# Key products of the next chunk pair traced between the two chunks of the current pair's scan

## The chip, the cores and the metric

One core of a Trainium2 chip runs the whole kernel; nothing is exchanged with other cores. The metric is the device time of one launch in microseconds (us), as the median of several runs.

## What is computed

Two layers of a backbone for a diffusion model, on 512 latent tokens and 256 context tokens of 1024 channels. Each layer has a mixer (an RWKV-7 recurrence in both directions, windowed attention, a Fourier mixer, merged by gates) and a gated ConvFFN. What this case touches is the recurrence, four heads of 64 channels, run forward and backward, over the context first and then over the latents:

```python
def wkv_scan(state0, feat, d, reverse):
    r, v, kk, decays, keys, removals, _ = feat

    def step(S, inp):
        r_t, w_t, k_t, v_t, kk_t, b_t = inp
        sa = jnp.einsum("bhvk,bhk->bhv", S, -kk_t)
        S = S * w_t[:, :, None, :] + sa[..., :, None] * b_t[..., None, :] + v_t[..., :, None] * k_t[..., None, :]
        return S, jnp.einsum("bhvk,bhk->bhv", S, r_t)

    xs = tuple(jnp.swapaxes(t, 0, 1) for t in (r, decays[d], keys[d], v, kk, removals[d]))
    S_last, y = lax.scan(step, state0, xs, reverse=reverse)
    return jnp.swapaxes(y, 0, 1), S_last
```

## The kernel before, in words

All activations stand with channels on the 128 partitions and tokens along the free dimension. The recurrence is done in chunks of 64 tokens, and two chunks of either direction make a *pair* (128 tokens). A layer has six pairs: w = 0 and 1 are the context, w = 2 to 5 the latents. Both directions and all heads of a pair go together. A pair has three parts.

- `wkv_features` (L779) computes the pair's operands for both directions d. Four small products a direction on TensorE (L814) give decay and gate; ScalarE takes tanh and exp; VectorE sums the decay along the chunk (L825) and multiplies the operands into the tiles W1 (L851 on VectorE, L853 on POOL) and BK (L854, L855). Then come the **key products**: for each direction and half of the partitions four products BK x W1 (L864) into one PSUM tile, whose masked copies go to MR (L869) and back into W1 (L870). POOL scales BK by the decay (L872).
- `wkv_inverse` inverts eight 64x64 unit triangular blocks that stand in MR. Its first half is VectorE's alone: a transpose of MR (L909), 30 small dependent steps that invert 16x16 blocks (L917 and L919, fifteen each), scaled copies (L924, L926) and two transposes (L929, L930). Its second half joins the blocks to 32 and to 64, by small products on TensorE (L938, L944, L948, L967, L974) and copies on VectorE and ScalarE between them (L940, L952, L957, L970, L977).
- `wkv_step`, once for each chunk j = 0, 1, carries the state: products L1021, copy L1024, products with the inverse L1028, copy L1031, products L1039, sum L1042 into the next chunk's state, and the outputs (L1047, L1052, L1063). `wkv_prep` (L987, L997) transposes a chunk's operands for it.

`wkv_scan` (L878) traces inverse, preparations and steps of pair w; before it the features of pair w + 1 are traced. All this is at high priority. At normal priority stands the *filler*: projections of the attention, Fourier and gate inputs, each of three products per weight tile (L177, L178, L179; 128x512, and in layer 0 128x256 too for the context), with weight splits on ScalarE (L106) and on POOL or VectorE (L118). The tile scheduler orders each engine's instructions by data, buffers and priority, and priority is the order of tracing; at run time each engine then works through its list in order. PSUM has two slots "x" for products, inverse and preparations and one slot "y" for the steps; MR has two buffers.

The run method's caller `mix` traces pair 0's scan before the projections and the others after them. What follows is built from the code:

Of the kernel before, what the change touches and what calls it, by code (L numbers as in the profile page):

```python
# [63 lines left out]
class Kern:  # L64
# [713 lines left out]

    def wkv_features(self, l, w, F, P, wp, wt):  # L779

        nc = self.nc
        x = P["x"]
        NC = 2
        WT = NC * CH
        W = {}
        MR = self.t(wp, [128, 4 * NC, 128], "MR", bufs=2)
        need_y = l == 0 or w > 1
        m = 128 if need_y else 64
        first = w in (0, 2, 3)
        part = "c" if w < 2 else "l"  # L790
        los = (w * WT, TC - (w + 1) * WT) if w < 2 else ((w - 2) * WT, TL - (w - 1) * WT)
        base = TL if w < 2 else 0

        def rows(t, h):
            return t[64 * h:64 * h + 64]

        for d in range(2):
            lo = base + los[d]

            def flip(s):  # L800
                return s[:, :, ::-1] if d else s

            def tok(t):
                return flip(t[:, :, lo:lo + WT])

            W1 = [self.t(wp, [128, NC, 2, 128], f"W1{h}", bufs=4) for h in range(2)]
            for h in range(2):

                nc.gpsimd.memset(rows(W1[h], 1 - h)[:, :, :, 0:m], 0.0)
            pp = self.ps()  # L810
            for z, (lw, xx) in enumerate(((P["w2"], F["xw"]), (P["a2"], F["xa"]))):
                for k in range(2):
                    c = (2 * z + k) * WT
                    nc.tensor.matmul(pp[:, c:c + WT], lhsT=lw[:, d, k * 128:(k + 1) * 128], rhs=xx[:, lo:lo + WT],  # L814
                                     start=True, stop=True)
            sw = self.t(wt, [128, 2, WT], "wt")
            ta = self.t(wt, [128, 2, WT], "wt")
            for z, (o, b, sc) in enumerate(((sw, 2 * d, 0.5), (ta, 4 + 2 * d, -0.5))):
                for k in range(2):
                    c = (2 * z + k) * WT  # L820
                    src = pp[:, c:c + WT]
                    self.act(o[:, k], src[:, ::-1] if d else src, AF.Tanh, scale=sc, bias=x[:, b + k:b + k + 1])
            self.sig(sw)
            L = self.t(wt, [128, 2, WT], "wt")
            nc.vector.tensor_tensor_scan(L.rearrange("p k t -> p (k t)"), self.smask, sw.rearrange("p k t -> p (k t)"),  # L825
                                         0.0, ALU.mult, ALU.add)

            kf = self.t(wt, [128, 2, WT], "wt")
            for k in range(2):
                self.act(kf[:, k], ta[:, k], AF.Identity, scale=x[:, 8 + k:9 + k], bias=x[:, 10 + k:11 + k])  # L830
            e1 = self.t(wp, [128, 2, NC, CH + 1], "e1", bufs=4)
            nc.gpsimd.memset(e1[:, :, :, 0:1], 1.0)
            self.act(e1[:, :, :, 1:], L.rearrange("p k (c t) -> p k c t", t=CH), AF.Exp, scale=-DECAY)
            e2 = self.t(wt, [128, 2, WT], "wt")
            self.act(e2, L, AF.Exp, scale=DECAY, bias=x[:, 25:26])
            nc.vector.tensor_tensor(kf, kf, tok(F["k"]), ALU.mult)
            na = ta
            nc.vector.scalar_tensor_tensor(na, ta, -1.0, tok(F["kk"]), ALU.add, ALU.mult)
            if need_y:
                kb = flip(F["kb" + part][:, :, los[d]:los[d] + WT])  # L840
                if first:
                    nc.gpsimd.tensor_copy(kb, kf)
                else:
                    nc.gpsimd.tensor_tensor(kb, kb, kf, ALU.add)
            BK = self.t(wp, [128, NC, 2, 128], "BK", bufs=4)
            split = lambda a: a.rearrange("p k (c t) -> p k c t", t=CH)
            for h in range(2):
                ww = rows(W1[h], h).rearrange("p c k t -> p k c t")
                bk = rows(BK, h).rearrange("p c k t -> p k c t")
                o = 64 * h  # L850
                nc.vector.tensor_tensor(ww[:, :, :, 0:64], split(rows(tok(F["kk"]), h)), rows(e1, h)[:, :, :, 0:64], ALU.mult)  # L851
                if need_y:
                    nc.gpsimd.tensor_tensor(ww[:, :, :, 64:128], split(rows(tok(F["r"]), h)), rows(e1, h)[:, :, :, 1:65], ALU.mult)  # L853
                nc.vector.tensor_tensor(bk[:, :, :, o:o + 64], split(rows(na, h)), split(rows(e2, h)), ALU.mult)  # L854
                nc.vector.tensor_tensor(bk[:, :, :, 64 - o:128 - o], split(rows(kf, h)), split(rows(e2, h)), ALU.mult)  # L855
            vs = self.t(wp, [128, 2, WT + CH], "vs_", bufs=4)
            nc.gpsimd.memset(vs[0:64, :, 0:64], 0.0)
            nc.gpsimd.memset(vs[64:128, :, WT:WT + 64], 0.0)
            self.act(vs[0:64, :, 64:64 + WT], tok(F["v"])[0:64])
            self.act(vs[64:128, :, 0:WT], tok(F["v"])[64:128])  # L860
            for h in range(2):
                ps = self.ps()
                for q in range(4):
                    nc.tensor.matmul(ps[:, q * 128:q * 128 + m], lhsT=BK[:, q // 2, q % 2, :],  # L864
                                     rhs=W1[h][:, q // 2, q % 2, 0:m], start=True, stop=True)
                pv = ps.rearrange("p (q t) -> p q t", q=4)[:, :, 0:m]
                oth = 1 - h
                mask = lambda z: rows(self.gmask, z)[:, 0:m].unsqueeze(1).broadcast_to((64, 4, m))
                nc.vector.tensor_tensor(rows(MR, h)[:, 4 * d:4 * d + 4, 0:m], rows(pv, h), mask(h), ALU.mult)  # L869
                nc.vector.tensor_tensor(rows(W1[h], oth).rearrange("p c k t -> p (c k) t")[:, :, 0:m], rows(pv, oth),  # L870
                                        mask(oth), ALU.mult)
            nc.gpsimd.tensor_tensor(  # L872
                BK, BK, e1[:, :, :, 64].rearrange("p k c -> p c k").unsqueeze(3).broadcast_to((128, NC, 2, 128)), ALU.mult)
            W[d] = (W1, BK, vs, e1)
        return w, W, MR, los

    def wkv_scan(self, l, win, then, F, S, wb):
        nc = self.nc  # L878
        w, W, MR, los = win
        NC = 2  # L880
        TTt = self.wkv_inverse(MR, wb)
        cur = S["cur"]
        if cur is None:
            cur = self.wkv_prep(0, W, wb)
            for h in range(2):
                nc.gpsimd.memset(cur[0][h][64 * h:64 * h + 64], 0.0)
        for j in range(NC):
            nxt = None
            if j + 1 < NC:
                nxt = self.wkv_prep(j + 1, W, wb)  # L890
            elif then is not None:
                nxt = self.wkv_prep(0, then[1], wb)
            self.wkv_step(l, w, j, F, W, MR, TTt, cur, nxt, wb, los)
            cur = nxt
        S["cur"] = cur

    def wkv_inverse(self, MR, wp):
# [431 lines left out]
    def mix(self, l, at, atp, W, pls, ring, A, B):  # L1329
# [7 lines left out]
        P = self.rwkv_params(l, rp)  # L1337
        F = {m: self.t(rp, [128, 2, TT], m) for m in ("r", "k", "v")}
# [26 lines left out]
        wa = self.pool("wa", side=B)  # L1365
        wt = self.pool("wt", bufs=6, side=B)
        wb = self.pool("wb", side=B)
        S = {"cur": None}
        with tc.high_priority():
            w0 = self.wkv_features(l, 0, F, P, wa, wt)  # L1370
            w1 = self.wkv_features(l, 1, F, P, wa, wt)
            self.wkv_scan(l, w0, w1, F, S, wb)

        stg = self.pool("stg", bufs=2 + l, side=B)
        cos = self.t(stg, [128, TL], "cos", bufs=1)
# [75 lines left out]
        work = fill()  # L1451
        with tc.high_priority():
            for w in range(2, 7):
                w0, w1 = w1, self.wkv_features(l, w, F, P, wa, wt) if w < 6 else None
                self.wkv_scan(l, w0, w1, F, S, wb)
            wb.release()
            wt.release()
            wa.release()
            tmp = self.pool("rtmp", side=B)
            self.rwkv_readout(l, F, P, y, tmp)  # L1460
            tmp.release()
# [346 lines left out]
```

## Time and profile before

| what | value |
|---|---|
| runs before | 2510.15 us median of 3 (2508.0 to 2512.45) |
| the profiled execution's own time | 2513.85 us |
| its span | 2511.9 us |
| TensorE busy (PE) | 2293.3 us, 91% |
| VectorE busy (DVE) | 1889.0 us, 75% |
| ScalarE (ACT), GpSimd (POOL) busy | 1052.8 and 965.1 us |
| mean granted TensorE clock | 0.965 |

PE is TensorE's matmuls and PEld its weight loads, DVE is VectorE, ACT ScalarE, POOL GpSimd. All times within the profile are counted from the start of its span. The scan of layer 0 lies at about 150 to 443 us and that of layer 1 at about 1541 to 1817 us. A granted clock of 1.00 is 2.4 GHz and one of 0.50 is 1.2 GHz; a mean over a stretch lies between them. In the rows, idle time before an instruction is followed by what ended it (the releaser). A row of the table of stretches gives its begin and end, its length, the busy time (and count of instructions) of PE, PEld, DVE, ACT and POOL, the mean granted clock, the DMA engines' busy share and GB/s. A row of a timeline gives start, duration, engine, line, operation, tiles and, in brackets, the idle time before it. A row of groups gives the count, then busy us and mean ns of one, then the idle us before them with its releasers. A row of waits gives who waited for whom, the sum of us, how often, and the longest.

### The profile page before, as it was taken

To read this page: it belongs to the slowest core of one execution; us is meant where nothing else is said; L and a number is where in the kernel's file an instruction comes from. 1 tells how busy PE (TensorE), PEld (TensorE's weight loads), DVE (VectorE), ACT (ScalarE), POOL (GpSimd) and SP (SyncE) were. 2 spreads that over 40 slices of the span, in tenths; PEclk is the share of its full clock that TensorE was granted. 3 is DMA by queue.
4 is the path that set the end of the run, shared out by engine and by line. 5 is a ranking of instruction groups with operands and counts; after the bars stand their busy time and mean duration, and the time that the engine had idled before them with its cause. 6 is when DMAs were issued, how large, how long until landed. Compare 5 with 4: busy or idle time off the path is not lost. (4 is left out here: it accounts for less than half of the span.)

```text
span 2511.9 us, 43604 instructions
## 1 busy us (share of the span) xinstructions
PE 2293.3 (91%) x16612; PEld 1923.1 (77%) x16612; DVE 1889.0 (75%) x3458; ACT 1052.8 (42%) x2153; POOL 965.1 (38%) x965
## 2 busy tenths in 40 slices
PE   7878999999999979999999989889889997899997
PEld 4757777887777768898898777667667776888886
DVE  4967777838866587778778854888667857989988
ACT  3234343335434444343333544435345434544443
POOL 4443322023332363333333544343224424644453
PEclk9989989999999989999999999899999998999999
DMA  7611111644334322222222322112275643322321
GB/s 241 190 51 47 57 37 46 204 146 122 118 122 125 104 67 65 63 72 68 64 69 66 122 93 63 54 59 61 76 211 149 195 128 113 117 88 85 98 89 59
DMA packets 284529, 251.36 MB, mean 100 GB/s; under 512 B 14524, under 2 KB 241300, under 8 KB 284320
## 3 DMA queue, kind: packets, MB, share of 16 engines
q1 hardware_dynamic: 284320, 248.58, 32.0%
q8 instruction: 131, 2.15, 0.4%
q14 instruction: 78, 0.64, 0.1%
HBM read 221.23 MB, written 27.29 MB: 99 GB/s over the span
## 5 line engine op out<-in xcount | busy, mean ns | idle before, releaser
L177 PE MATMUL mm<-at,wh 128*128 128x256 f32 (+2 forms) x1968 | 661.8, 337 | 14.4 <-DVE v L614 7.0
L178 PE MATMUL mm<-at,wh 128*128 128x256 f32 (+2 forms) x1968 | 660.5, 336 | 12.8 <-POOL at L118 7.3
L179 PE MATMUL mm<-at,wl 128*128 128x256 f32 (+2 forms) x1968 | 659.7, 336 | 8.2 <-DVE wl L118 5.9
L118 POOL TENSOR_TENSOR wl<-wr,wh 128x512 fp32r<-128x512 f32 (+1 forms) x248 | 341.8, 1385 | 466.2 <-ACT wh L106 444.0
L177 PEld LDWEIGHTS mm<-at,wh 128*128 128x128 f32 x1968 | 380.8, 194 | 46.9 <-issue 5.6
L178 PEld LDWEIGHTS mm<-at,wh 128*128 128x128 f32 x1968 | 381.1, 194 | 43.4 <-POOL at L118 10.0
L179 PEld LDWEIGHTS mm<-at,wl 128*128 128x128 f32 x1968 | 380.9, 194 | 34.4 <-DVE wl L118 8.9
L106 ACT ACTIVATE wh<-wr 128x512 fp32r<-128x512 f32 (+1 forms) x342 | 204.9, 605 | 235.2 <-PE mm L178 141.3
L118 DVE TENSOR_TENSOR wl<-ws,wh 128x512 fp32r<-128x512 f32 x176 | 166.8, 949 | 65.6 <-ACT wh L106 65.6
L177 PE MATMUL x<-dh,hid 128*128 128x512 f32 x440 | 178.0, 405 | 29.8 <-DVE acc L604 27.7
L295 DVE SCALAR_TENSOR_TENSOR ma<-mw,s,ma 128x256 f32<-128x256 f32 x336 | 187.3, 597 | 11.0 <-DMA mw<-in_mod_w 8.2
L179 PE MATMUL x<-dh,hid 128*128 128x512 f32 x440 | 173.3, 395 | 1.0 <-DVE hid L118 1.0
L178 PE MATMUL x<-dl,hid 128*128 128x512 f32 x440 | 173.2, 394 | 0.0
L604 DVE TENSOR_TENSOR acc<-x,acc 128x512 f32<-128x512 f32 x200 | 134.4, 682 | 24.2 <-PE x L179 23.7
L118 POOL TENSOR_TENSOR dl<-dr,dh 128x1024 fp32r<-128x1024 f32 x44 | 112.2, 2549 | 83.9 <-ACT dh L106 83.9
L106 ACT ACTIVATE wh<-ws 128x512 fp32r<-128x512 f32 x170 | 103.7, 623 | 84.9 <-PE mm L178 70.5
L177 PEld LDWEIGHTS x<-dh,hid 128*128 128x128 f32 x440 | 83.3, 189 | 56.4 <-DVE acc L604 38.6
L154 POOL TENSOR_TENSOR ws<-wr,wr 128x512 f32<-128x512 f32 x42 | 66.4, 1580 | 139.5 <-DVE wl L118 136.9
L178 PE MATMUL x<-at,wh 128*128 128x512 f32 (+2 forms) x312 | 114.4, 367 | 5.0 <-POOL at L118 3.1
L177 PE MATMUL x<-at,wh 128*128 128x512 f32 (+2 forms) x312 | 114.7, 368 | 0.9 <-DVE wh L114 0.7
L106 ACT ACTIVATE P<-P,st 128x513 f32<-128x513 f32 (+5 forms) x120 | 86.0, 722 | 69.8 <-DVE P L1234 58.6
L154 POOL TENSOR_TENSOR ws<-ws,wr 128x512 f32<-128x512 f32 x42 | 62.8, 1495 | 132.5 <-DVE wl L118 75.0
(490 smaller groups left out, 4859.0 us busy)
## 6 DMA issues: line engine op xcount, KB each, us to landing
mw<-in_mod_w SPq DMA_DIRECT2D x96, 512.0 KB, 4.1
wr<-in_ffn_up SPq DMA_DIRECT2D x176, 256.0 KB, 3.1
wr<-in_w_in SPq DMA_DIRECT2D x164, 256.0 KB, 3.0
dr<-in_ffn_down SPq DMA_DIRECT2D x44, 512.0 KB, 3.3
gd<-sg SPq DMA_DIRECT2D x32, 256.0 KB, 2.0
wraw<-in_w_out SPq DMA_DIRECT2D x32, 256.0 KB, 3.7
hd<-h SPq DMA_DIRECT2D x32, 256.0 KB, 2.4
h<-hd SPq DMA_DIRECT2D x28, 256.0 KB, 6.7
```

The costliest lines, as they stand in the source:

```text
L106: return self.nc.scalar.activation(out, in_, func, **kw)
L118: e.tensor_tensor(lo, full, hi.bitcast(F32), ALU.subtract)
L154: e.tensor_tensor(raw[m], raw[x], raw[y], op)
L177: mm(ps, lhsT=lh, rhs=rh, start=first and k == 0, stop=False)
L178: mm(ps, lhsT=lh, rhs=rl, start=False, stop=False)
L179: mm(ps, lhsT=ll, rhs=rh, start=False, stop=last and k == nk - 1)
L295: nc.vector.scalar_tensor_tensor(acc[s], mw[:, k % 4], v, acc[s], ALU.mult, ALU.add)
L604: nc.vector.tensor_tensor(acc[i][:, cs], ps, acc[i][:, cs], ALU.add)
```

## The change

`wkv_features` becomes a generator with two parts. It stops once the operand tiles W1, BK, vs and e1 of both directions are made, and the caller goes on with that. The key products, their evacuations into MR and W1 and the scaling of BK are its second part. For pair 0 the second part is traced at once. For every other pair `wkv_scan` traces it after the first of the two steps of the pair before. No operation is added or left out.

```diff
--- before.py
+++ after.py
@@ -778,6 +778,7 @@
 
     def wkv_features(self, l, w, F, P, wp, wt):
 
+
         nc = self.nc
         x = P["x"]
         NC = 2
@@ -858,6 +859,10 @@
             nc.gpsimd.memset(vs[64:128, :, WT:WT + 64], 0.0)
             self.act(vs[0:64, :, 64:64 + WT], tok(F["v"])[0:64])
             self.act(vs[64:128, :, 0:WT], tok(F["v"])[64:128])
+            W[d] = (W1, BK, vs, e1)
+        yield w, W, MR, los
+        for d in range(2):
+            W1, BK, _, e1 = W[d]
             for h in range(2):
                 ps = self.ps()
                 for q in range(4):
@@ -871,10 +876,9 @@
                                         mask(oth), ALU.mult)
             nc.gpsimd.tensor_tensor(
                 BK, BK, e1[:, :, :, 64].rearrange("p k c -> p c k").unsqueeze(3).broadcast_to((128, NC, 2, 128)), ALU.mult)
-            W[d] = (W1, BK, vs, e1)
-        return w, W, MR, los
-
-    def wkv_scan(self, l, win, then, F, S, wb):
+
+    def wkv_scan(self, l, win, then, rest, F, S, wb):
+
         nc = self.nc
         w, W, MR, los = win
         NC = 2
@@ -892,6 +896,8 @@
                 nxt = self.wkv_prep(0, then[1], wb)
             self.wkv_step(l, w, j, F, W, MR, TTt, cur, nxt, wb, los)
             cur = nxt
+            if j == 0:
+                self.advance(rest, 1)
         S["cur"] = cur
 
     def wkv_inverse(self, MR, wp):
@@ -1367,9 +1373,12 @@
         wb = self.pool("wb", side=B)
         S = {"cur": None}
         with tc.high_priority():
-            w0 = self.wkv_features(l, 0, F, P, wa, wt)
-            w1 = self.wkv_features(l, 1, F, P, wa, wt)
-            self.wkv_scan(l, w0, w1, F, S, wb)
+            f0 = self.wkv_features(l, 0, F, P, wa, wt)
+            w0 = next(f0)
+            self.advance(f0, 1)
+            f1 = self.wkv_features(l, 1, F, P, wa, wt)
+            w1 = next(f1)
+            self.wkv_scan(l, w0, w1, f1, F, S, wb)
 
         stg = self.pool("stg", bufs=2 + l, side=B)
         cos = self.t(stg, [128, TL], "cos", bufs=1)
@@ -1451,8 +1460,9 @@
         work = fill()
         with tc.high_priority():
             for w in range(2, 7):
-                w0, w1 = w1, self.wkv_features(l, w, F, P, wa, wt) if w < 6 else None
-                self.wkv_scan(l, w0, w1, F, S, wb)
+                f1 = self.wkv_features(l, w, F, P, wa, wt) if w < 6 else None
+                w0, w1 = w1, next(f1) if w < 6 else None
+                self.wkv_scan(l, w0, w1, f1, F, S, wb)
             wb.release()
             wt.release()
             wa.release()
```

The built programs show where the instructions go. The lists below are each engine's own, in its order; the change shifts line numbers after L779 by up to ten, so L915 is the former L909, L946 the former L940, L983 the former L977, L1037 the former L1031, L874 and L875 the former L869 and L870.

VectorE, layer 1, the start of the scan, before: the evacuations of pair 0's first direction (`MR`, `W`), the features of its second one (`wt`, `kk`, `BK`). L1148 and L1150 are filler.

```order
L869 TENSOR_TENSOR MR_15447<-x_15488,table_539 64x4x64
L870 TENSOR_TENSOR W_2990_15448<-x_15488,table_539 64x4x64
L869 TENSOR_TENSOR MR_15447<-x_15495,table_539 64x4x64
L870 TENSOR_TENSOR W_2991_15449<-x_15495,table_539 64x4x64
L1148 TENSOR_TENSOR mm_16118<-mm_16118,sin_15986 128x512
L1150 TENSOR_TENSOR stg_15988<-stg_15988,mm_16118 128x512
L726 TENSOR_SCALAR wt_15512<-wt_15512 128x256
L825 SCALAR_TENSOR_TENSOR wt_15519<-smask_543,wt_15512 128x256
L836 TENSOR_TENSOR wt_15521<-wt_15521,k_14903 128x256
L838 SCALAR_TENSOR_TENSOR wt_15513<-wt_15513,kk_15416 128x256
L851 TENSOR_TENSOR W_3003_15503<-kk_15416,e_3010_15524 64x2x2x64
L854 TENSOR_TENSOR BK_15531<-wt_15513,wt_15527 64x2x2x64
```

After, the same place:

```order
L855 TENSOR_TENSOR BK_15516<-wt_15498,wt_15512 64x2x2x64
L856 TENSOR_TENSOR BK_15516<-wt_15506,wt_15512 64x2x2x64
L874 TENSOR_TENSOR MR_15447<-x_15528,table_539 64x4x64
L875 TENSOR_TENSOR W_2990_15448<-x_15528,table_539 64x4x64
L874 TENSOR_TENSOR MR_15447<-x_15535,table_539 64x4x64
L875 TENSOR_TENSOR W_2991_15449<-x_15535,table_539 64x4x64
L1154 TENSOR_TENSOR mm_16118<-mm_16118,sin_15986 128x512
L874 TENSOR_TENSOR MR_15447<-x_15543,table_539 64x4x64
L875 TENSOR_TENSOR W_3001_15488<-x_15543,table_539 64x4x64
L874 TENSOR_TENSOR MR_15447<-x_15550,table_539 64x4x64
L875 TENSOR_TENSOR W_3002_15489<-x_15550,table_539 64x4x64
L915 STREAM_TRANSPOSE iv_15639<-MR_15447 128x512
```

The second direction's features are done before the first evacuation, all of pair 0's evacuations follow each other, and the transpose L915 that starts its inverse comes right behind them. Before, that transpose stood behind the second direction's features and its own evacuations.

VectorE, layer 1, the end of the inverse of pair 4 and the step it feeds, before: `TTt_17852` is that inverse, `itmp` and `T_3405` belong to the small steps of pair 5's inverse, and `XV` is written by the first step.

```order
L977 COPY TTt_17852<-x_17946 32x8x32
L917 TENSOR_TENSOR itmp_18136<-F_3404_18134,T_3405_18135 128x63
L919 TENSOR_TENSOR T_3405_18135<-T_3405_18135,itmp_18136 128x9x7
L917 TENSOR_TENSOR itmp_18136<-F_3404_18134,T_3405_18135 128x64
L919 TENSOR_TENSOR T_3405_18135<-T_3405_18135,itmp_18136 128x8x8
L917 TENSOR_TENSOR itmp_18136<-F_3404_18134,T_3405_18135 128x63
L1031 COPY XV_3334_17622<-y_18008 64x256
L919 TENSOR_TENSOR T_3405_18135<-T_3405_18135,itmp_18136 128x7x9
L917 TENSOR_TENSOR itmp_18136<-F_3404_18134,T_3405_18135 128x60
L919 TENSOR_TENSOR T_3405_18135<-T_3405_18135,itmp_18136 128x6x10
```

After, the same place (`TTt_17822` is pair 4's inverse, `MR_17690` belongs to pair 5):

```order
L946 COPY Ps_17826<-x_17827 128x128
L958 SCALAR_TENSOR_TENSOR iv_17823<-x_17827,table_539,iv_17823 32x8x16 x2
L963 COPY TTt_17822<-x_17827 16x8x16
L976 COPY Pb_17915<-x_17916 32x256
L963 COPY TTt_17822<-x_17827 16x8x16
L983 COPY TTt_17822<-x_17916 32x8x32
L1037 COPY XV_3334_17622<-y_17978 64x256
L874 TENSOR_TENSOR MR_17690<-x_18028,table_539 64x512
L875 TENSOR_TENSOR W_3343_17691<-x_18028,table_539 64x512
L1048 TENSOR_TENSOR ZV_3378_17958<-y_17999,Zp_17973 64x256
L1048 TENSOR_TENSOR ZV_3379_17959<-y_17999,Zp_17973 64x256
```

No small step of the next inverse stands among the copies of this one any more. The evacuations of pair 5's key products, which its inverse reads, now stand behind the first step's copy into `XV`.

TensorE, layer 1, the second half of pair 4's inverse, before (`mm` is filler, `x_17857` and `x_17946` are the inverse's PSUM tiles):

```order
L938 MATMUL x_17857<-iv_17853,MR_17247 32x16 x32
L178 MATMUL mm_18878<-at_14639,wh_18874 128x512
L179 MATMUL mm_18878<-at_14638,wl_18875 128x512
L177 MATMUL mm_18878<-at_14640,wh_18874 128x512
L178 MATMUL mm_18878<-at_14641,wh_18874 128x512
L944 MATMUL x_17857<-Ps_17856,TTt_17852 32x16 x16
L948 MATMUL x_17857<-TTt_17852,Ps_17856 16x16 x32
L179 MATMUL mm_18878<-at_14640,wl_18875 128x512
L177 MATMUL mm_18878<-at_14642,wh_18874 128x512
L178 MATMUL mm_18878<-at_14643,wh_18874 128x512
L179 MATMUL mm_18878<-at_14642,wl_18875 128x512
L967 MATMUL x_17946<-iv_17853,MR_17247 32x32
```

After, the same place:

```order
L177 MATMUL mm_18958<-at_14644,wh_18954 128x512
L178 MATMUL mm_18958<-at_14645,wh_18954 128x512
L179 MATMUL mm_18958<-at_14644,wl_18955 128x512
L944 MATMUL x_17827<-iv_17823,MR_17247 32x16 x32
L950 MATMUL x_17827<-Ps_17826,TTt_17822 32x16 x16
L954 MATMUL x_17827<-TTt_17822,Ps_17826 16x16 x32
L973 MATMUL x_17916<-iv_17823,MR_17247 32x32 x16
L980 MATMUL x_17916<-TTt_17822,Pb_17915 32x32 x16
L993 MATMUL x_17953<-ident_61,vs__3292_17286 128x128 x2
L993 MATMUL x_17953<-ident_61,vs__3303_17329 128x128 x2
L1034 MATMUL y_17978<-q_3386_17987,TTt_17822 64x64
```

Before, filler stands between the inverse's products to the end of the scan: 20 such matmuls from the first L938 to the last L1028 of pair 4. After, there are 15 in pairs 1 to 3 and none in pairs 4 and 5: the matmul ahead of pair 4's inverse is the last of the 516 of layer 1's scan, of which 165 stand ahead of the first inverse. In layer 0 the order has 673 filler matmuls up to the end of the scan before, 721 after, and 89 of them now stand between the products of pair 0 and its inverse.

## Rows read from the trace of the kernel before

**Rows 1.** The page's first part: busy us, share of the span, instructions

```profile
PE 2293.3 (91%) x16612; PEld 1923.1 (77%) x16612; DVE 1889.0 (75%) x3458; ACT 1052.8 (42%) x2153; POOL 965.1 (38%) x965
```

**Rows 2.** Table of stretches, both scans

```profile
150.20:227.00 76.80, 57.21 (x538) 48.11 (x538) 63.53 (x141) 30.12 (x75) 30.05 (x41) 0.87 0.15 49
...
227.00:411.70 184.70, 170.35 (x2222) 138.58 (x2223) 137.14 (x328) 75.03 (x196) 63.73 (x116) 0.93 0.14 44
...
1541.00:1623.00 82.00, 69.35 (x552) 56.22 (x550) 58.33 (x138) 35.56 (x78) 26.85 (x29) 0.83 0.19 59
...
1746.20:1786.30 40.10, 37.63 (x522) 28.90 (x522) 35.38 (x87) 19.76 (x51) 13.92 (x24) 1.00 0.19 61
```

**Rows 3.** VectorE's groups, 1746.2 to 1786.2

```profile
L118 DVE TENSOR_TENSOR wl<-wr,wh 128x512 fp32r<-128x512 f32 x6 | 4.4, 730 | 0.3 <-issue 0.2
L917 DVE TENSOR_TENSOR itmp<-F,T 128x60 f32<-128x60 f32 (+7 forms) x15 | 3.4, 225 | 0.5
L919 DVE TENSOR_TENSOR T<-T,itmp 128x63 f32<-128x63 f32 (+7 forms) x15 | 3.2, 216 | 0.5
...
L869 DVE TENSOR_TENSOR MR<-x,table 64x512 f32<-64x512 f32 x4 | 2.7, 686 | 1.3 <-PE x L864 1.3
...
L825 DVE TENSOR_TENSOR_SCAN wt<-smask,wt 128x256 f32<-128x256 bf16 x2 | 1.4, 688 | 0.0
...
L1024 DVE COPY q<-y 128x256 f32<-128x256 f32 x2 | 0.8, 415 | 0.8 <-PE y L1021 0.8
```

**Rows 4.** VectorE's timeline, layer 1, inverse of pair 4 and its step

```profile
1755.56 1.09 DVE L929 STREAM_TRANSPOSE iv<-iv 128x512 f32<-128x512 f32 x1
...
1776.18 0.27 DVE L940 COPY Ps<-x 128x128 f32<-128x128 f32 x1
...
1786.26 0.42 DVE L1031 COPY XV<-y 64x256 f32<-64x256 f32 x1 [0.23 <-PE y L1028]
```

**Rows 5.** Table of stretches, L940 to L1031, covered by the next inverse

```profile
355.68:370.08 14.40, 13.15 (x206) 9.81 (x205) 7.87 (x26) 5.55 (x14) 0.80 (x4) 0.65 0.17 48
402.93:411.65 8.72, 8.72 (x210) 7.23 (x209) 7.52 (x26) 4.40 (x11) 0.00 (x0) 1.00 0.21 64
...
1776.18:1786.26 10.08, 10.08 (x205) 7.22 (x204) 8.86 (x31) 4.41 (x11) 0.00 (x0) 1.00 0.26 81
```

**Rows 6.** The same stretch in the last pair of layer 1 and of layer 0

```profile
1795.86:1807.19 11.33, 11.23 (x262) 8.50 (x262) 3.99 (x12) 4.62 (x12) 2.79 (x5) 1.00 0.16 49
422.73:432.86 10.13, 10.13 (x249) 8.06 (x248) 3.24 (x11) 3.75 (x10) 1.52 (x4) 1.00 0.09 29
```

**Rows 7.** Who VectorE waited for, 1541 to 1623: us in total, times, longest

```profile
DVE kk L775 <- ACT kk L106: 6.4, 1, 6.4
DVE MR L869 <- PE x L864: 6.3, 6, 2.1
DVE mm L1148 <- PE mm L1147: 2.8, 1, 2.8
```

**Rows 8.** TensorE's groups in the scan of layer 0, 150.2 to 443

```profile
L864 PE MATMUL x<-W,BK 128*128 128x128 f32 x192 | 30.8, 326 | 22.8 <-DVE BK L855 12.8 <-POOL W L853 6.4 <-DVE BK L854 3.6
...
L948 PE MATMUL x<-TTt,Ps 32*16 32x16 f32 x384 | 4.8, 176 | 3.9 <-issue 3.9
```

**Rows 9.** TensorE's timeline: two starts of each width of filler

```profile
152.30 0.28 PE L177 MATMUL mm<-at,wh 128*128 128x256 f32 x1
152.42 0.28 PE L178 MATMUL mm<-at,wh 128*128 128x256 f32 x1
...
1702.07 0.39 PE L177 MATMUL mm<-at,wh 128*128 128x512 f32 x1
1702.30 0.40 PE L178 MATMUL mm<-at,wh 128*128 128x512 f32 x1
```

**Rows 10.** VectorE's timeline, layer 0: start of an inverse, its last transpose but one

```profile
180.57 1.10 DVE L909 STREAM_TRANSPOSE iv<-MR 128x512 f32<-128x512 f32 x1
...
211.18 1.08 DVE L929 STREAM_TRANSPOSE iv<-iv 128x512 f32<-128x512 f32 x1
```

## The prediction

> **What bounds the kernel now.** The page's first part comes first: TensorE is busy for 91% of the span and VectorE for 75% [rows 1]. That is a mean over many stages, and the change touches only the two scans, so the second view is the table of stretches over both of them [rows 2]. In layer 1 VectorE sets the pace: in the stretch 1746.2 to 1786.3, from one pair's L1031 to the next, it is busy for 35.38 of 40.1 us and idle for 4.7. In layer 0 TensorE does: from 227.0 to 411.7 it is busy for 170.35 of 184.7 us, since there the filler (the projections at L177 to L179, traced at normal priority) has 128x512 and 128x256 products, and after the scan filler is left for it to go on with. So the change is costed on VectorE's idle time in layer 1, and on TensorE's in layer 0.
>
> The third view, VectorE's groups of one pair's period, shows what fills the 35.4 us [rows 3]: the 30 small steps of the inverse (L917, L919) alone are 6.6 us, and the evacuations of the key products cost 1.3 us of waiting. The fourth is VectorE's timeline [rows 4], and it holds the point of this case: the second half of an inverse, which hands small blocks back and forth between TensorE and VectorE, begins at L940 (1776.18), and the step it feeds runs at L1031 (1786.26), but the first half of that inverse ended long before, with L929 at 1755.56. Before the change the inverse runs a pair ahead. Its first half fills the idle time of the pair before it, and this is why VectorE is busy for 8.86 of the 10.08 us from L940 to L1031 [rows 5]. The last pair has no next inverse to fill with: the same stretch took 11.33 us with VectorE busy for 3.99, so 7.34 idle where the covered one has 1.2 [rows 6].
>
> **The change part by part.** It adds and removes no instruction of weight. Its 16 key products a pair (L864), eight evacuations (L869, L870) and two scalings on POOL (L872) are only moved; no DMA and no new wait on SP's queue is among them. What moves is told by the order shown above, in four terms.
>
> *1. The inverses lose their cover (layer 1).* An inverse needs MR, which L869 writes. Now these writes stand behind L1031 of the step before, so the next inverse can't start in that step, and from its L940 to its L1031 VectorE's order has none of the next pair's small steps left. Five of the six inverses are newly bare (the last was already). Each goes from 1.2 us idle to 7.34: 5 x 6.1 = 30.5 us. In three of them the order has two weight splits (L118, about 0.73 us each) in the gap, which gives 4.4 back. The bounds of such a stretch: 8.72 us was the shortest (layer 0, large matmuls at full clock) and 14.40 the longest [rows 5], so with 4 us of own work between 4.7 and 10.4 idle. I take 7.34 since that row is the only one of layer 1 without cover; the ends are worth -13 and +15 for five.
>
> *2. What that buys on VectorE.* The evacuations come when the features are long done, so the waits of L869 (1.3 us) and of the second L1024 (0.8) go in four pairs: -8.4 us [rows 3]. At the start of the scan six waits of L869 sum to 6.3 us [rows 7]; about 1.7 remain, for the first of them: -4.6. The second direction's first three feature operations (L825 is 0.69 of them, and two shorter) are now ahead of L775, inside its 6.4 us of waiting [rows 3, 7]: -1.4. A further 2.8 us behind the rotary product L1148 [rows 7] stay, because L1148 still stands between the first evacuations.
>
> Layer 1: 30.5 - 4.4 - 8.4 - 4.6 - 1.4 = +11.7, say **+12 us**. The filler is 516 large matmuls in either order. But 351 of the 516 now stand between the first and the fifth inverse, and none behind: in the last two pairs TensorE has nothing large to do. This costs nothing by itself where VectorE is the limit; the work behind the scan (the readout) waits for the scan's end.
>
> *3. TensorE in layer 0.* L864 was waited for in 22.8 us and L948, behind it, in 3.9 [rows 8]. Of L864's waits the first, 3.6 us on L854, stays; 19.2 + 3.9 = 23.1 us go. New waits take their place. In front of the first L938 stand 89 filler matmuls; large ones start 0.23 us apart and half-width ones 0.12 [rows 9], so 89 x 0.175 = 15.6 us. VectorE needs 31.7 us from L909 to the end of L929 [rows 10], less 6.6 for the second pair's evacuations and their wait that are now elsewhere: 25.1. With some 1.5 us of feature products TensorE waits for 8 us, and for 2 more in the bare half: 10. Five further inverses have about 15 filler matmuls among them where 20 stood. A TensorE wait in such a stretch is between 0.9 us (five half-and-half matmuls) and 7.3 (as long as VectorE's); I take 3, nearer the low end, because the bare row of layer 1 has TensorE busy for 11.23 of 11.33 [rows 6]. That is 15. Layer 0: 10 + 15 - 23.1 = **+2 us**. The 48 filler matmuls more that its scan now holds are work moved ahead, neither gain nor loss.
>
> *4. TensorE's clock.* The granted clock was 0.87 and 0.83 in the two starts, 0.93 in layer 0's middle and 1.00 from 1746.2 to 1786.3 [rows 2]; 1.00 is the 2.4 GHz level and a mean below it holds some of 1.2. The stretch that took 14.40 us had a mean of 0.65; at 1.00 it took 8.72 and 10.08 [rows 5]. So a fall inside the inverse costs about 4.3 us against 10.1. Before a fall the engine had waited or worked only on small blocks. I count no change, since the starts lose waits of L864 while the inverses gain some.
>
> The Trainium skill, page "TensorE: Matmul & The Clock Gate", section "HAM oscillation — how this bites in real kernels", speaks against this change: idle gaps between bursts of matmuls bring the clock down again and again, and each burst then starts cold. By that rule the inverses would run at the lower level, and the sum would be nearer +50 than +14. The trace agrees in part: one of the three stretches of [rows 5] fell, two ran at 1.00 throughout. As a mechanism of this kernel it is the second rival below, with its price from the rows.
>
> **The sum.** 12 + 2 = +14 us. The profiled execution took 2513.85 us (span 2511.9), 3.7 more than the median 2510.15 of three; against that median the forecast is **2524 us**, slower by 0.6%. A measurement of this kernel can tell some 0.2%, 5 us, from no change.
>
> **The rivals.**
> *Faster, 2496.* The inverse is short and the waits that go aren't paid back. For it: products ready in time end 22.8 us of waiting for L864 in layer 0, and the first step starts some 12 us sooner in layer 1, since the second pair's evacuations (2.7 us) and half of its small steps (3.3) [rows 3] no longer stand ahead and 6 us of waits are gone (4.6 and 1.4 above). If TensorE waits only before the first inverse, layer 0 gives 10 - 23.1 = -13; if each bare stretch takes 8.72 us, layer 1 gives 12 - 13 = -1. Sum -14. Against it: the only bare stretches of the trace, 11.33 and 10.13 us [rows 6], had VectorE idle for about 7. It decides for itself where the idle time of a pair in layer 1 stays below about 7 us (now 4.7).
> *Clock, 2545.* Every bare inverse leaves TensorE with small blocks, and in layer 1's last two pairs without filler. If five of the twelve stretches more than before pay the 4.3 us: +21 on the forecast. For it: the 0.65 [rows 5] and the 0.83 of the start, which has a first inverse with little filler. Against it: 1.00 in the bare stretches of both layers [rows 6].
> *No change, 2510.* The terms cancel: layer 0 gains what layer 1 loses, for example 3 us less a stretch than I take in both layers (layer 1 about +3, layer 0 about -3 with TensorE waiting 2 us a pair).
> That the change doesn't do what it says is ruled out by the order: the evacuations stand behind L1031.
>
> **How the numbers follow.** Forecast (2516 to 2534 by itself) 0.42, clock 0.16, no change 0.20, faster 0.22. So slower by over 0.2% is 0.58, within 0.2% 0.20, faster 0.22. The time predicted is the likeliest, 2524. The range reaches to the faster rival and to the clock rival, 2496 to 2545; a tenth lies beyond each end, where a bound is passed in both layers.
>
> **What would show it.** In the profile of the changed kernel the waits of L864 (its new line is 869) for BK should be nearly gone in both layers. In VectorE's timeline the stretch from L946 to L1037 (now L940 to L1031) should be bare in every pair, 10 to 12 us with about 7 idle. The distance of one pair's first L1037 from the next should be about 43 us in layer 1, where it was 40; the last pair's, 20.9 before (from 1786.26 to 1807.19, the end of the bare stretch), should grow by more than the 6.6 us of small steps that are now inside it. The last two pairs of layer 1 should have no large matmul between their steps. Wrong would be the forecast if VectorE were as idle per pair as before, if the scan of layer 1 took no longer than before, or if the difference lay in a stage behind the scans.

## The result and the profile after

The change made the kernel slower: 2592.78 us (median of 4 runs, 2587.28 to 2596.2) against 2511.3 us for the kernel before in the same comparison, a ratio of 1.0323 with a 95% interval of 1.0300 to 1.0346. The sign was forecast, the size was not: +14 us were predicted and +81 measured, outside the range. The profiled execution has a span of 2585.3 us, 73.4 more than before.

The page's first part after, to be read against [rows 1]:

```profile
PE 2332.7 (90%) x16612; PEld 1960.4 (76%) x16612; DVE 1889.9 (73%) x3458; ACT 1052.1 (41%) x2153; POOL 962.0 (37%) x965
```

The work is the same: as many instructions on every engine, and VectorE (DVE) is busy for 0.9 us more. TensorE (PE) needed 39.4 us more for the same 16612 matmuls, and the mean granted clock is 0.935 where it was 0.965. In the rest of the 73 us it waited.

Where they lie, by the times of the first step's copy into `XV` (L1037, before L1031) in VectorE's timeline: from pair 0 to pair 5 layer 0 took 244.9 us instead of 205.9 (+39.0), layer 1 242.3 instead of 184.2 (+58.2). Both scans start earlier, by 7.8 and 7.6 us, and layer 0 gets 9 us back behind its scan, where less filler is left. The stages outside the scans took as long as before, within some 5 us. So in the profile the forecast's +2 us of layer 0 became +22, and its +12 us of layer 1 became +51.

The table of stretches after, first from L1037 to L1037: pairs 0 to 4 of layer 0, one pair of layer 1 (1693.16), the last (1843.74). Then from L946 (before L940) to L1037: layer 1's pair 2 (1729.81) and pair 4 (1834.15), layer 0's last (454.95). The columns are those of [rows 2]. `...` stands for lines left out:

```profile
219.17:430.96 211.79, 186.28 (x2255) 154.10 (x2255) 146.71 (x346) 77.51 (x202) 66.03 (x118) 0.84 0.14 45
...
1693.16:1745.14 51.98, 46.23 (x480) 36.14 (x480) 35.94 (x88) 20.83 (x50) 13.41 (x28) 0.83 0.20 62
...
1843.74:1878.93 35.19, 22.69 (x432) 19.20 (x432) 22.67 (x64) 6.83 (x18) 5.11 (x10) 0.65 0.01 1
...
1729.81:1745.14 15.33, 15.33 (x200) 10.53 (x200) 3.01 (x9) 5.23 (x13) 0.79 (x4) 0.50 0.18 54
...
1834.15:1843.74 9.59, 7.80 (x185) 6.43 (x185) 2.33 (x9) 3.17 (x9) 0.33 (x1) 0.50 0.19 59
...
454.95:464.09 9.14, 9.14 (x203) 6.89 (x203) 2.33 (x8) 3.77 (x10) 0.00 (x0) 1.00 0.09 32
```

A pair of layer 1 takes 52 us where it took 40 [rows 2], and VectorE does the same work in it, 35.94 us: it is idle for 16.0 us instead of 4.7. Of these, 12.3 lie in the second half of the inverse, which is bare (3.01 us of work in 15.33) as forecast. But it was forecast at 11.33 us [rows 6]. The clock there is 0.50, the 1.2 GHz level, throughout. VectorE's timeline of the same pair shows the rest of the 52 us:

```profile
1693.16 0.42 DVE L1037 COPY XV<-y 64x256 f32<-64x256 f32 x1 [3.67 <-PE y L1034]
...
1700.77 0.68 DVE L875 TENSOR_TENSOR W<-x,table 64x512 f32<-64x512 f32 x1
...
1701.71 1.04 DVE L915 STREAM_TRANSPOSE iv<-MR 128x512 f32<-128x512 f32 x1
...
1727.43 1.07 DVE L935 STREAM_TRANSPOSE iv<-iv 128x512 f32<-128x512 f32 x1
...
1729.81 0.28 DVE L946 COPY Ps<-x 128x128 f32<-128x128 f32 x1
...
1745.14 0.42 DVE L1037 COPY XV<-y 64x256 f32<-64x256 f32 x1 [3.67 <-PE y L1034]
```

Step, key products and evacuations (8.5 us), first half (25.7 to its transpose), transposes (2.4), second half (15.3), step: the five links add up to the whole period. Nothing in the loop lies beside another link any more. Before, the loop had no such sum, since two inverses were under way at once. In VectorE's timeline of the kernel before, pair 4's inverse begins 49.9 us ahead of the L1031 that it serves (1786.26 [rows 4]), in a period of 40:

```profile
1736.39 1.04 DVE L909 STREAM_TRANSPOSE iv<-MR 128x512 f32<-128x512 f32 x1
```

What stands ahead of the low clock is shown by TensorE's timeline, in layer 1's pair 2 and in layer 0's last pair:

```profile
1723.32 0.39 PE L177 MATMUL mm<-at,wh 128*128 128x512 f32 x1
1728.55 1.05 PE L944 MATMUL x<-iv,MR 32*32 32x16 f32 x64 [4.84 <-DVE iv L935]
...
454.16 0.73 PE L944 MATMUL x<-iv,MR 32*32 32x16 f32 x64 [0.78 <-DVE iv L935]
```

TensorE has run through the filler that its order puts ahead of L944 and waits 4.84 us for VectorE's transpose. Eleven of the twelve second halves begin with such a wait, of 2.9 to 9.7 us, and from their first product to L1037 the mean clock is 0.50 to 0.70. In nine of them it was at 0.50 when the first product ran, in the other two within 0.9 us. The twelfth is the last of layer 0: it waits 0.78 us and runs at 1.00, in 9.14 us, with 19 filler matmuls among its products; the others have 15 to 27, or none in layer 1's last two pairs. TensorE's own waits in the two scans, summed:

```profile
PE x L944 <- DVE iv L935: 33.5, 6, 9.7
...
PE x L869 <- DVE BK L855: 3.6, 1, 3.6
...
PE x L944 <- DVE iv L935: 28.9, 6, 7.3
```

The first two rows are layer 0 and the third is layer 1. The waits of layer 0's key products that the change was to end are gone as forecast (3.6 us left of 22.8 [rows 8]); 33.5 us of new ones stand in their place.

### The profile page after: what moved, and what is told of

Read it like the earlier page. It is cut to its first block, busy times and chain, and to the rows that moved or that the text cites. A ratio compares the mean times of both kernels' runs of the same rounds, so it can differ in the third digit from the quotient of the medians.

```text
span 2585.3 us, 43651 instructions
## 1 busy us (share of the span) xinstructions
PE 2332.7 (90%) x16612; PEld 1960.4 (76%) x16612; DVE 1889.9 (73%) x3458; ACT 1052.1 (41%) x2153; POOL 962.0 (37%) x965
## 5 line engine op out<-in xcount | busy, mean ns | idle before, releaser
L177 PE MATMUL mm<-at,wh 128*128 128x256 f32 (+2 forms) x1968 | 668.7, 340 | 13.7 <-DVE v L614 6.4
L178 PE MATMUL mm<-at,wh 128*128 128x256 f32 (+2 forms) x1968 | 668.1, 340 | 13.4 <-POOL at L118 7.2
L179 PE MATMUL mm<-at,wl 128*128 128x256 f32 (+2 forms) x1968 | 666.9, 339 | 13.6 <-DVE wl L118 10.2
L177 PEld LDWEIGHTS mm<-at,wh 128*128 128x128 f32 x1968 | 386.5, 197 | 46.9 <-ACT wh L106 5.4
L178 PEld LDWEIGHTS mm<-at,wh 128*128 128x128 f32 x1968 | 386.6, 196 | 44.9 <-POOL at L118 10.0
L179 PE MATMUL x<-at,wl 128*128 128x512 f32 (+2 forms) x312 | 113.6, 364 | 0.0
```

Source lines behind the costliest of these rows:

```text
L177: mm(ps, lhsT=lh, rhs=rh, start=first and k == 0, stop=False)
L178: mm(ps, lhsT=lh, rhs=rl, start=False, stop=False)
L179: mm(ps, lhsT=ll, rhs=rh, start=False, stop=last and k == nk - 1)
```

## The experiments

Theory A: the products' place behind step 0 makes one chain of what were two overlapping inverses, and TensorE's wait in that chain costs the clock on top. Its rivals were the clock alone (B), the new order of the features, which comes with the split into two parts (C), and the way through step 0 alone (D).

| kernel | us | ratio to before (95% interval) |
|---|---|---|
| changed kernel | 2592.78 | 1.0323 (1.0300 to 1.0346) |
| second part ahead of the inverse | 2497.72 | 0.9956 (0.9938 to 0.9975) |
| second part behind the inverse | 2569.77 | 1.0246 (1.0221 to 1.0270) |
| features late too | 2560.73 | 1.0205 (1.0188 to 1.0222) |
| small added matmuls | 2550.88 | 1.0166 (1.0146 to 1.0185) |
| slots only | 2587.86 | 1.0310 (1.0278 to 1.0341) |
| start only | 2509.17 | 1.0005 (0.9986 to 1.0024) |
| before, with small matmuls | 2529.50 | 1.0076 (1.0051 to 1.0101) |
| ahead of the inverse, with small matmuls | 2526.04 | 1.0075 (1.0047 to 1.0102) |
| features late, with small matmuls | 2572.30 | 1.0257 (1.0237 to 1.0276) |
| late in layer 1 only | 2563.09 | 1.0223 (1.0196 to 1.0250) |

**The place.** One line moves:

```diff
+        self.advance(rest, 1)
         TTt = self.wkv_inverse(MR, wb)
...
-            if j == 0:
-                self.advance(rest, 1)
```

> The changed kernel, with the second part (key products, evacuations) traced at the head of the scan, ahead of the inverse of the pair before, as it lay before the change; the split into two parts and the new start stay. In VectorE's order the next inverse's small steps stand again in the second half of the current one. Theory A (the loss is that the next inverse can't start before step 0: products, first half, second half and step have become one chain, and TensorE's waits before each second half bring the clock down there): 2485 to 2515 us, the second halves 10 to 11 us at a clock of 1.00 and the period of layer 1 about 40. Rival C (that both directions' features now come first, ahead of any product, is what costs): over 2550.

It took 2497.72 us. Three stretches of it, the period of pairs 1 to 2 in layer 1 and the second halves of pairs 3 and 4:

```profile
1656.32:1696.56 40.24, 35.43 (x462) 27.45 (x463) 37.91 (x97) 20.32 (x51) 13.50 (x28) 1.00 0.24 74
1723.67:1737.08 13.41, 12.58 (x203) 8.61 (x202) 8.56 (x26) 4.84 (x13) 0.80 (x4) 0.75 0.34 100
1765.38:1774.52 9.14, 9.05 (x201) 6.53 (x200) 8.28 (x25) 4.44 (x12) 0.00 (x0) 1.00 0.45 137
```

VectorE is busy for 8.3 to 8.6 us in these second halves again, and the period is 40. So neither the split nor the features' order costs anything; the place alone is worth 95 us, and this version (below: the early version) is faster than the kernel before too, by 0.4%. The expected clock of 1.00 held in seven of the twelve second halves; the other five ran at 0.61 to 0.89, among them the one of 13.41 us.

**Behind the inverse, ahead of step 0.**

```diff
         TTt = self.wkv_inverse(MR, wb)
+        self.advance(rest, 1)
...
-            if j == 0:
-                self.advance(rest, 1)
```

> The second part traced right after the inverse of the pair before, ahead of step 0. In VectorE's order the eight evacuations stand behind the second half and ahead of the first L1031 of step 0, and the second half is still bare. Theory A: the chain loses only the step and its copies (4 to 5 us of about 52 a pair), so 2545 to 2575 us, second halves still about 15 us with the clock at 0.50 to 0.60. Rival D (only the way through step 0 made the loss, the bare second half costs little): below 2530.

2569.77 us, as Theory A has it for the time. One pair of layer 1, from one first copy into `XV` to the next, then its second half:

```profile
1682.44:1730.09 47.65, 42.87 (x475) 33.52 (x475) 36.94 (x90) 20.29 (x50) 13.71 (x29) 0.86 0.24 73
1712.00:1730.09 18.09, 18.09 (x234) 14.13 (x234) 8.43 (x17) 3.31 (x8) 2.30 (x4) 0.71 0.15 45
```

The step leaves the chain, the rest of it stays: the next inverse begins 0.3 us behind the copy into `XV`. The second halves were not the 15 us expected. They take 18.1 to 20.8 us in pairs 2 to 4 of layer 1, at 0.59 to 0.71, since the evacuations now stand in them. D falls.

**Features late.**

```diff
         TTt = self.wkv_inverse(MR, wb)
+        then = next(rest) if rest is not None else None
+        S["next"] = then
...
```

> The changed kernel with the first part too (the features of the next pair) traced later, after the inverse of the current pair and ahead of its step 0. In VectorE's order the first half then has no feature operations among its small steps, and some 11 of them stand between the second half's last copy and L1031. Theory A: the first half falls from 25 us to 13 to 17 in layer 1, the chain to 43 to 47 us a pair, total 2520 to 2560. Rival B (the loss is TensorE's clock alone): TensorE still waits before each second half, the clock stays at 0.50 there, total 2580 to 2600.

2560.73 us, 0.7 us above the range. A pair of layer 1, then the first and second half in it:

```profile
1664.91:1713.03 48.12, 44.82 (x470) 34.56 (x470) 36.09 (x88) 19.87 (x48) 11.94 (x27) 0.82 0.22 67
1677.60:1692.70 15.10, 14.76 (x104) 11.35 (x103) 13.82 (x47) 6.00 (x12) 1.57 (x4) 1.00 0.41 123
1694.60:1713.03 18.43, 18.43 (x214) 13.56 (x215) 8.22 (x21) 7.45 (x22) 1.74 (x6) 0.54 0.15 44
```

The first half fell from 25.7 to 15.1 us as expected, but the features now stand between the second half's last copy and `XV`, and it grew to 18.4; the period is 48 and not the 43 to 47 hoped for. The stretch from `XV` to the transpose that starts the next inverse grew too, from 8.5 to 12.7 us, since features stand in it. So 10.6 us came off one link, 3.1 and 4.2 went onto two others, and the chain is 3.9 us shorter. Rival B falls by the time; the clock, though, stayed low as it had said, with shorter waits (below).

**The clock alone.** Seven small matmuls an inverse, each of which can start only when a small step is done, split TensorE's one wait:

```diff
-        tmp = self.t(wp, [128, 64], "itmp", bufs=1)
+        hb = self.ps("hb")
...
+            tmp = self.t(wp, [128, 64], "itmp", bufs=2)
...
+            if q in (2, 4, 6, 8, 10, 12, 14):
+                for _ in range(1):
+                    mm(hb[0:n * m, 0:128], lhsT=tmp[:, 0:n * m], rhs=self.ident, start=True, stop=True)
...
-            self.banks(dict(x=2, y=1), dict(mm=5))
+            self.banks(dict(x=2, y=1, hb=1), dict(mm=4))
```

> The changed kernel with seven small matmuls added to each inverse (128 columns, lhsT is the product of a small step, written to a PSUM slot of their own, taken from the filler's five), one after every second small step, so that TensorE's filler is spread along the first half and its one wait before the second half (3 to 10 us) is cut into short ones. If the clock falls because of that wait, the second halves run at 0.90 to 1.00 and take 10 to 12 us instead of 15 to 17. Theory A (chain and clock): the period of layer 1 goes from 52 to 46 to 48 us, total 2530 to 2555. Rival B (clock alone): back to the time before, 2505 to 2520. Rival E (the clock only mirrors small blocks and sets no time): 2585 to 2610, for the added matmuls.

2550.88 us. A pair of layer 1, its second half, and that of the last pair; behind them, TensorE's timeline ahead of the second half:

```profile
1661.35:1706.66 45.31, 41.07 (x485) 30.27 (x486) 35.72 (x87) 20.40 (x51) 13.54 (x28) 1.00 0.23 70
1697.17:1706.66 9.49, 9.49 (x201) 6.80 (x202) 3.71 (x10) 4.77 (x13) 0.80 (x4) 1.00 0.28 83
1825.04:1834.63 9.59, 7.76 (x184) 6.32 (x184) 2.32 (x7) 3.17 (x9) 0.00 (x0) 0.50 0.02 3
```

```profile
1681.75 0.42 PE L929 MATMUL hb<-ident,itmp 128*55 128x128 f32 x2 [1.84 <-DVE itmp L924]
...
1694.54 0.39 PE L929 MATMUL hb<-ident,itmp 128*15 128x128 f32 x2
...
1696.39 0.73 PE L948 MATMUL x<-iv,MR 32*32 32x16 f32 x64
```

The wait of 4.84 us is gone (L948 is the former L944), the longest left in the pair is 1.84. Second halves with the same products and 15 or 16 filler matmuls take 8.8 to 9.5 us instead of 15.3, and eleven of twelve run at 0.94 or more. The first half is as long as it was (25.9 us against 25.7), so in this pair the wait itself had cost the chain nothing. The period falls by 6.7 to 45.3. It does not fall to 40: the chain is still there. So of the 81 us, 42 went with the clock, net of the added matmuls, and about 40 stayed. Rivals B and E fall.

The control leaves the matmuls out and keeps the slots:

```diff
-            self.banks(dict(x=2, y=1), dict(mm=5))
+            self.banks(dict(x=2, y=1), dict(mm=4))
```

> Control for the run with the small added matmuls: the changed kernel with the filler's PSUM slots cut from five to four and nothing added. Theory A (the added matmuls kept the clock up by cutting TensorE's wait): the waits before the second halves and the low clock in them stay, 2580 to 2605 us. Rival F (fewer filler slots alone rearranged the filler and ended the waits): 2545 to 2560.

2587.86 us, with waits of 2.7 to 9.4 us ahead of eleven second halves and their clock at 0.50 to 0.64. So it was not the slots (F falls). The second buffer of `itmp`, which came with the matmuls, was not tried alone.

**The start alone**, in the kernel before: pair 0's products of both directions behind the features of both.

```diff
...
+            for dd in (range(0) if w == 0 and d == 0 else range(2) if w == 0 else (d,)):
+                self.key_products(W[dd], MR, m, dd)
...
```

`key_products` holds the moved lines.

> The kernel before with one part of the change alone: for pair 0 the key products of both directions stand behind the features of both; for all other pairs nothing moves. If the gain of the early-placed version (2498 us, most of it there by the first step of pair 1 in layer 1) comes from the start, 2495 to 2504 us. If it comes from features ahead of products in every pair, 2507 to 2513.

2509.17 us, no difference. By elimination the 13 us of the early version come from features ahead of products in the other pairs too: its first period of layer 1 is 36.9 us where it was 44.2, later ones are about as before.

**The same small matmuls where the overlap exists**: in the kernel before, and in the early version (the edit is the one above).

> The kernel before with the seven small matmuls added to each inverse, in a PSUM slot taken from the filler. Here the first half lies beside another pair's second half, and ten of twelve second halves ran at 0.76 to 1.00 already. Theory A: little is left to win and 84 matmuls of about 0.3 us are paid, some of them in TensorE's way between the second half's products: 2500 to 2530 us. Rival B (clock alone): as much as in the changed kernel, 2470 to 2490.

> The early-placed version (2498 us) with the seven small matmuls in each inverse. Five of its twelve second halves ran at 0.61 to 0.89. If they rise to 1.00 and give back 4 to 5 us each: 2478 to 2490 us. If the added matmuls, which wait for a small step in TensorE's order, hold up the second half beside them: 2500 to 2525.

2529.50 and 2526.04 us, so some 20 and 28 us slower than without. The first is within what Theory A said; the second is 1 us above the slower of its two ranges, and the hope (2478 to 2490) was wrong. In the early version with them all six second halves of layer 0 ran at 1.00, and still it lost. Over all runs the mean clock hardly rose, from 0.964 to 0.966.

Where the loss comes from is not shown. TensorE's waits for the 84 small matmuls (about 0.4 us each) sum to 1.2 us in the first and 4.8 in the second, so the queue held up by them is a small part. From the first `XV` to the last, layer 0 took 8.6 and 7.8 us less than without them; the stretch from there to layer 1's first `XV` took 17.3 and 14.5 more, and layer 1's scan 5.8 and 8.8 more. In the early version the second halves of pairs 1 and 2 in layer 1 took 14.6 and 15.3 us from first product to L1037, where 12.3 and 10.8 stood, but their clock was 0.77 and 0.78 instead of 1.00, and none of the small matmuls lies in the first of them. The filler's missing fifth slot was not tried alone in these two kernels.

**Both remedies in the changed kernel** (the two edits together):

> Both remedies at once: features traced after the inverse (alone it took the changed kernel from 2593 to 2561 us) and the small added matmuls (alone 2593 to 2551). Theory A holds that the chain's length and the clock are two accounts: the gains of 32 and 42 us add to about 2519, 2510 to 2530 us, with second halves at 1.00. If they were one account, won twice over (the late features only shortened TensorE's wait): 2545 to 2560.

2572.30 us, slower than with either alone, and outside both expectations. Second halves of layer 1's pairs 2 and 3:

```profile
1713.40:1731.11 17.71, 17.00 (x224) 13.56 (x223) 8.25 (x21) 7.88 (x23) 2.92 (x7) 0.71 0.15 46
1761.50:1776.01 14.51, 13.85 (x226) 10.37 (x227) 8.64 (x21) 9.47 (x27) 3.34 (x7) 1.00 0.13 38
```

Even at 1.00 the second half takes 14.5 us, with 8.64 us of VectorE's work in it since the features stand there, so the clock had less to give; and in layer 0 the distance from the first `XV` to the last grew from 235.4 us to 244.7, against features late alone. So the two gains are not independent. Which part of the loss is the added matmuls' own and which the order's stays open.

**By layer:**

```diff
+        if l == 0:
+            self.advance(rest, 1)
         TTt = self.wkv_inverse(MR, wb)
...
-            if j == 0:
+            if j == 0 and l == 1:
```

> The second part traced at the head of the scan in layer 0 (as in the version of 2498 us) and after step 0 in layer 1 alone. By the traces the changed kernel lost about 50 us in layer 1 and 23 in layer 0 against the kernel before, and the early version won 9 in layer 1 and nothing in layer 0. If the layers add: 2555 to 2568 us. If layer 1 starts otherwise because of layer 0's order: outside of that.

2563.09 us, within the range: the layers add. Layer 1's share against the early version is some 65 us, layer 0's the other 30.

## Why the prediction was wrong, point by point

Two steps failed. Term 4 put the clock at nothing, and 42 of the 81 us went when the clock was kept up. Term 1 priced one link of the loop, the bare second half, where the whole loop had become serial: with the clock kept up about 40 us stayed, and 14 were forecast.

- **Term 1, the bare second halves: right that they are bare, too small as a price.** It gave each 7.34 us of idle VectorE, hence 6.1 more than before. In the changed kernel it was some 12 idle in pairs 1 to 3 of layer 1, and these pairs took some 12 us more each. With the clock kept up by the small matmuls the periods from pair 1 to pair 4 were 45.3 to 46.9 us, 5.8 to 6.9 more than before. That is near the 6.1, but the forecast took gains and weight splits off it and expected a period of about 43. The row it was taken from [rows 6] was a second half that TensorE entered without a wait.
- **Term 1 also stopped at L940.** The last pair's period went from 20.9 to 35.2 us: with no features left, its first half is bare too (15.2 us from the last evacuation to L946, 13.26 of them VectorE's own work) and nothing of it lies beside pair 4 any more. Its second half, 10.6 us at 0.50, is no longer than the 11.33 at 1.00 that it was [rows 6], so these 14 us are the chain's and not the clock's. The prediction named this as a sign to look for, at more than 6.6 us, and had no price for it in the sum.
- **Term 2, the gains: mostly not there.** Of -8.4 us the wait for the second step's operand went, but evacuations still wait 1.6 us a pair for products, since nothing lies between. The start was as good as said, 7.6 us sooner where 6.0 were forecast.
- **Term 3: the waits removed were right (L864), those in their place too small.** 25 us were counted in layer 0, 10 for the first inverse and 3 for each later one. The first was 9.7. Four of the five later ones are 5.4 to 6.1 us, the last 0.8, the sum of all six 33.5; layer 0 lost 22 us in all (39.0 less 7.8 at the start and 9 behind the scan) and not 2. In layer 1 TensorE's waits were taken as free. Their 28.9 us cost little as time, but the clock was low behind them.
- **Term 4: wrong.** "I count no change" failed. The rival's price of 4.3 us a fall was near (5.8: 15.33 against 9.49). Its count was short: four second halves of the kernel before had a mean clock of 0.65 to 0.86 between L940 and L1031, of which [rows 5] shows one; eleven have 0.50 to 0.72 there now. So seven more fell and not five, and the four fell further. Its chance was 0.16. The error was to look at the bare stretches of the kernel before for the clock and not at the wait ahead of them, which the change creates. Its sentence on what TensorE did before a fall does not fit either: in those four second halves 4 to 13 filler matmuls stood between the first product and the fall, with waits of 1.4 us at most.
- **The rule of the Trainium skill**, page "TensorE: Matmul & The Clock Gate", section "HAM oscillation — how this bites in real kernels", bore out in sign: gaps between bursts bring the clock down again and again. The trace agrees, with waits of 2.9 to 9.7 us ahead of eleven slow second halves and 0.78 ahead of the fast one. It does not cover every fall, as the last section shows. What was won by keeping the clock up was 42 us, by the run with small matmuls. The prediction shows no working for its +50.
- **The rivals:** the faster one was wrong (VectorE is idle for 16.0 us a pair in layer 1 where under 7 would have decided for it); the clock rival was right in kind; no change is excluded by the +81; the order did what it said.

## What to carry to other kernels

In a software pipeline, trace what feeds the next round's long serial part ahead of the current round's wait, even if that makes an engine wait for it: here 23 us of TensorE's waits were worth less than the overlap that they kept. Before moving work, write down the loop of dependent links and add it up; if the sum exceeds the period, the overlap is what you live on. And when an engine order leaves TensorE waiting ahead of a block of small products, price that block at the lower clock, with all the filler in it.

## What the runs showed of the chip

The granted clock decided how long a second half took. These two rows run from the first product of a second half to the copy into `XV`, in layer 1's pair 2 of the changed kernel and in pair 3 of the one with small matmuls, both with 264 matmuls, 15 of them filler:

```profile
1728.55:1745.14 16.59, 16.59 (x264) 11.75 (x264) 4.27 (x10) 5.23 (x13) 0.79 (x4) 0.50 0.17 50
...
1742.67:1752.74 10.07, 10.07 (x264) 7.39 (x264) 4.27 (x10) 4.87 (x13) 0.79 (x4) 1.00 0.19 59
```

TensorE is busy all the time in both. Being busy did not bring the clock back within the first: the granted clock stayed at 0.50 for all of the 16.59 us. At 0.50 and without filler (layer 1's pair 4) L946 to L1037 took 9.59 us, where 15.33 stood with 15 filler matmuls. So at the low clock the large matmuls that stand in the queue among the small ones made 5.7 us of it. A second half at 1.00 without filler did not occur.

A wait directly ahead was not needed for a fall. In the kernel before, layer 0's pair 3 enters its second half at 1.00 without a wait, and the clock falls 5.3 us later:

```profile
354.58:359.86 5.28, 4.03 (x176) 3.55 (x175) 4.19 (x9) 0.90 (x2) 0.48 (x1) 1.00 0.20 57
359.86:370.08 10.22, 10.22 (x98) 7.33 (x98) 4.75 (x19) 4.65 (x12) 0.80 (x4) 0.50 0.14 40
```

In the run with both remedies layer 1's pair 2 did the same, at 1.00 for 4.8 us and then at 0.50, a mean of 0.73. Nor did the length of a wait tell: with features late, seven second halves came behind waits of 1.0 to 2.2 us, and five of them ran at 0.56 to 0.64 and two at 1.00. Small matmuls did not help the last pair, which has no filler and ran at 0.50. What else brings the clock down there was not settled.
